# The last two chunks of a feed-forward projected up by seven products of halves

## The chip, the cores and the metric

The kernel runs on one core of a Trainium2 chip. The metric is the device time of one execution in microseconds; before the change the median of three runs is 2227.38 us. The engines named here are TensorE (PE in the profile, its weight loads PEld), VectorE (DVE), ScalarE (ACT), GpSimd (POOL) and SyncE (SP, which issues most loads).

## The reference, cut to what matters

The network has two layers over 512 tokens of width 1024. Each layer has a SwiGLU feed-forward, a mixer, a second feed-forward and a gated embedding, and after each of them a normalised residual. The change is in the feed-forwards, of which there are four; hidden width is 2816.

```
def swiglu_ffn(x, w_gu, w_d):
    g, u = jnp.split(x @ w_gu, 2, axis=-1)
    return (jax.nn.silu(g) * u) @ w_d
...
x = layer_norm(DN_ALPHA * x + 0.5 * swiglu_ffn(x, ffn1_wgu[i], ffn1_wd[i]), ln_g[i, 0], ln_b[i, 0])
```

Everything is float32.

## The kernel before, in words

**Float32 by three products.** A float32 operand is kept as two parts, a high part that is rounded to the matmul's type by a ScalarE copy, and a low part, the rest, which VectorE makes by a subtraction (`split`, and lines 198 and 207 for weights). `mm3` (lines 279 to 281) makes three matmuls of each product: high by high, high by low, low by high. So each weight tile costs one ScalarE and one VectorE instruction of 128 x 1024 elements before TensorE may use it.

**One feed-forward.** The hidden width is 22 blocks of 128, taken in chunks of 2, 4, 4, 4, 4 and 4 blocks (`FFN_CHUNKS`; chunk 0 to chunk 5). For each block there are two projections up, gate and up half: 8 input blocks by three matmuls of 512 tokens, 24 matmuls into one PSUM bank (`up`, the tile fps). ScalarE applies Silu to the gate (sg), VectorE multiplies it by the up half into h. The activations stand transposed in xh and xl (high and low part, 8 input blocks by 512 tokens).

**The product down** of a chunk is done one chunk later, woven into the next chunk's projections, by the class `Group`: seven products of halves (a Strassen form) in place of eight. Each product needs one form of h (`form`: VectorE sums, then a split into fhi and flo) and one form of the down weights (kind "rows", `forms`). One product is 12 matmuls of 512 columns (the tile gps), and its result is added to the residual xt by two VectorE additions (`add`). The order in a chunk is: projection, product, projection, product, and so on, seven products within eight projections. The last chunk's down product is not woven: it is plain rows of weights after the chunk (`down`, the tile dps).

**Weights.** The class `Weights` holds an order of all weight tiles, and splits the next one when a buffer is free. There are four buffers of kind "main" and three of kind "rows". `release` after a product gives a buffer back and at once issues the split of the tile that is next in the order, so a tile's split is issued when the product that stands four main tiles ahead has been issued, and waits for that product's matmuls. Raw weights come by DMA into three buffers of 1 MB (wraw) and five of 512 KB (wquarter). Elsewhere in the kernel, in the mixers, `release(low="dma")` makes the low part without VectorE: ScalarE writes the negated copy, and a GpSimd DMA adds the raw weights to it in place (line 205).

**What sets the order.** Every engine's queue is written out by the program (`manual_schedule`): instructions stand in the order in which the Python code calls them, and wait on semaphores for what they read and overwrite. There are four banks for projections and four for the down side.

Of the kernel before, what the change touches and what calls it, by code (L numbers as in the profile page):

```python
# [10 lines left out]
F32 = mybir.dt.float32  # L11
# [33 lines left out]
PLE_EXTRA = 3  # L45


class Weights:
# [4 lines left out]
    def __init__(self, nc, raw_pool, split_pool):  # L53
        self.nc = nc
        self.pools, self.free = {"main": split_pool}, {"main": W_BUFS, "none": 0}
        self.raw_pools, self.raw_bufs = {"raw": raw_pool}, {"raw": RAW_BUFS}
        self.raw_free, self.raw_at, self.raw_tags = deque(range(RAW_BUFS)), {}, {}
        self.loads, self.left, self.raws = [], [], {}
        self.queues, self.held_raws = defaultdict(deque), defaultdict(deque)
        self.order, self.next_split, self.in_place = [], 0, set()  # L60
        self.ready, self.taken, self.held = deque(), deque(), []
# [34 lines left out]
    def forms(self, kind, b11, b12, b22, b21):  # L96
# [25 lines left out]
        return [(kind, js, make) for js, make in made]  # L122

# [50 lines left out]
    def fill(self, most=1000, low=None, meanwhile=None):  # L174

        while most and self.next_split < len(self.order):
# [19 lines left out]
            for i in range(parts):  # L196
                s = slice(i * shape[1] // parts, (i + 1) * shape[1] // parts)
                self.nc.scalar.activation(hi[:, s], src[:, s], AF.Copy)  # L198
                if meanwhile and make in self.in_place:
                    meanwhile()  # L200
                    meanwhile = None
                if low == "dma" and make not in self.in_place:

                    self.nc.scalar.activation(lo[:, s], src[:, s], AF.Copy, scale=-1.0)
                    self.nc.gpsimd.dma_start(lo[:, s], src[:, s], accum_op=OP.add)
                else:
                    self.nc.vector.tensor_sub(lo[:, s], src[:, s], hi[:, s].bitcast(F32))  # L207
# [41 lines left out]
def hybrid_trunk(ctx: ExitStack, tc, x, p, ln_g, ln_b, ffn1_wgu, ffn1_wd, ffn2_wgu, ffn2_wd,  # L249
# [39 lines left out]
    def up_bank(name):  # L289
        up_order.rotate(-1)  # L290
        return ps_up.tile([P, 512], F32, name=name, tag=f"up{up_order[-1]}")
# [56 lines left out]
    LAST = len(FFN_CHUNKS) - 1  # L348
    turn_p = []

    def ffn_weights(wgu, wd, name, ple=False):
# [12 lines left out]
        for at in range(HB):  # L364
            if at in (0, HB - 1):
                W.add(*((kp(wgu)[:, :, c0:c0 + P], [slice(None)]) for c0 in (at * P, HID + at * P)))
            elif at % 2:
                add_pairs(wgu, at * P, HID + at * P)
        tiles = W.order[first:]
        del W.order[first:]  # L370
        for c, n in enumerate(FFN_CHUNKS):
            down_w = deque(forms(c - 1) if c else ())
            for i in range(2 * n):
# [5 lines left out]
        add_rows(wd, starts[LAST], 4, ["rows", "rows", "main", "main"] if ple else ["main", "rows", "rows", "rows"])  # L379
# [74 lines left out]
    def ple_weights(i):  # L454
        add_rows(ple_wp[i], 0, 2)
        add_wide(ple_wg[i], 0, ["extra", "extra", "extra", "main"])
        add_wide(ple_wg[i], 512, ["rows", "rows", "rows", "rows2"])
# [196 lines left out]
    def down(hs, first, norm=None, lazy=False, defer=False):  # L654
# [5 lines left out]
        def release(k):  # L660
            kind = "rows" if kinds[k] == "rows" else None
            if norm is None:
                W.release(kind=kind)
            elif kind == "rows":
# [162 lines left out]
    def ffn(layer, k, rows, prepare=None):  # L827
        with stage_pool("forms", 2) as fpool, stage_pool("quarters", Q_BUFS) as qpool, stage_pool("hpool", 2) as hpool:
# [14 lines left out]
            group, hs = None, []  # L843
            for c, n in enumerate(FFN_CHUNKS):
# [4 lines left out]
                for i in range(2 * n):  # L849
# [20 lines left out]
                    if c == 1 and i < 3:  # L870
                        run_affine()
                if c < LAST:
# [5 lines left out]
                if c == 1:  # L878
                    norm = Norm(layer, k)
            return down(hs, False, norm, lazy=layer == 0, defer=prepare is not None)  # L880

    def ffn_stage(layer, k):
        with stage_pool("rows", 3) as rows:
            W.open("rows", rows, 3)
            ffn(layer, k, rows)
            W.close("rows")

# [572 lines left out]
    def ffn_ple(i, last):  # L1460
        with stage_pool("rows", 3) as rows:
            W.open("rows", rows, 3)
# [18 lines left out]
            finish = ffn(i, 2, rows, load_p)  # L1481
            with stage_pool("extra", PLE_EXTRA) as extra, stage_pool("rows2") as rows2, stage_pool("ple2") as mp:
# [68 lines left out]
                for kind in ("rows", "rows2", "extra"):  # L1551
# [55 lines left out]
```

## Time and profile before

| | before |
|---|---|
| median of 3 runs | 2227.38 us (2226.92 to 2227.43) |
| profiled execution, span | 2225.4 us, granted TensorE clock 0.999 |
| TensorE busy | 2214.4 us in 10517 matmuls |
| VectorE, ScalarE, GpSimd busy | 1557.3, 922.2, 104.3 us |
| VectorE and ScalarE, 214.5 to 340 us (chunks 4 and 5 of the first feed-forward) | 80.5 and 44.2 of 125.5 us |
| moved by DMA | 253.57 MB, mean 114 GB/s |

A row of a group or of the timeline names line, engine, operation, output and inputs (buffer numbers left out), and shapes; a timeline row begins with its start and its duration in microseconds, and a bracket at its end gives the idle time ahead of it and who ended it. Matmuls overlap, so their price is the distance between two starts, not their duration. In the answers by windows each row has the stretch, its length, the busy time of TensorE, its weight loads, VectorE, ScalarE and GpSimd (with counts), the granted clock, the mean busy share of the 16 DMA engines, and GB/s.

### The profile page before, as it was taken

What the parts mean: (1) busy time and instruction counts of PE and PEld (TensorE: products, weight loads), DVE (VectorE), ACT (ScalarE), POOL (GpSimd) and SP (SyncE); (2) the same over time, 40 slices, a digit from 0 to 9 for tenths busy, and PEclk for the clock granted to TensorE, in tenths of its full rate; (3) what the DMA queues carried; (4) which work ended last, traced back from release to release, by engine and by line L of the source; (5) the groups of instructions that cost most, each with busy time, mean ns of one, the idle gap of its engine ahead of it and who ended that gap; (6) DMA issues with size and microseconds to landing.
All of it is one profiled execution on the core that took longest, in us unless ns stands there. A gap on an engine that the chain in (4) does not pass through costs nothing.

```text
span 2225.4 us, 26475 instructions
## 1 busy us (share of the span) xinstructions
PE 2214.4 (100%) x10517; PEld 1856.1 (83%) x10517; DVE 1557.3 (70%) x2280; ACT 922.2 (41%) x1308; POOL 104.3 (5%) x135
## 2 busy tenths in 40 slices
PE   9999999999999999999999999999999999999998
PEld 8888888888888888888888888888888888888887
DVE  5666667776776786666687766666788778666677
ACT  4333336464646443333345333335345453333332
POOL 1000000111101100000000000000001100000000
PEclk9999999999999999999999999999999999999999
DMA  7422223466847444332233422223437743332221
GB/s 230 130 95 88 95 86 100 100 143 140 160 117 154 130 133 128 98 106 63 99 123 111 134 92 90 95 85 97 140 76 152 164 129 130 117 114 86 85 86 57
DMA packets 206308, 253.57 MB, mean 114 GB/s; under 512 B 5812, under 2 KB 160564, under 8 KB 206184
## 3 DMA queue, kind: packets, MB, share of 16 engines
q1 hardware_dynamic: 168080, 211.83, 29.4%
q0 software_dynamic: 31488, 25.35, 8.4%
q10 hardware_dynamic: 6616, 14.69, 2.0%
q8 instruction: 83, 1.36, 0.2%
q14 instruction: 41, 0.34, 0.0%
HBM read 224.58 MB, written 2.11 MB: 102 GB/s over the span
## 4 chain that ended last, share of the span: by engine, by line
PE 98%; ACT 1%; DMA 0%; DVE 0%; issue 0%; SPq 0%; DVEq 0%
PE fps L279 13%; PE fps L280 13%; PE fps L281 13%; PE gps L279 8%; PE gps L281 8%; PE gps L280 8%; PE dps L279 2%; PE dps L281 2%; PE dps L280 2%; PE gups L279 1%; PE vps L279 1%; PE zps L279 1%; PE zps L281 1%; PE vps L281 1%; PE gvps L279 1%; PE gups L280 1%
## 5 line engine op out<-in xcount | busy, mean ns | idle before, releaser
L279 PE MATMUL fps<-xh,whi 128*128 128x512 f32 x1312 | 510.7, 389 | 0.0
L280 PE MATMUL fps<-xl,whi 128*128 128x512 f32 x1312 | 510.4, 389 | 0.0
L281 PE MATMUL fps<-xh,wlo 128*128 128x512 f32 x1312 | 510.4, 389 | 0.0
L207 DVE TENSOR_TENSOR wlo<-wraw,whi 128x1024 fp32r<-128x1024 f32 (+1 forms) x292 | 352.7, 1218 | 147.9 <-ACT whi L198 146.8
L198 ACT ACTIVATE whi<-wraw 128x1024 fp32r<-128x1024 f32 (+1 forms) x340 | 352.2, 1048 | 179.0 <-PE fps L280 81.6
L207 DVE TENSOR_TENSOR wlo<-wquarter,whi 128x1024 fp32r<-128x1024 f32 (+1 forms) x140 | 156.5, 1118 | 218.2 <-ACT whi L198 218.2
L281 PEld LDWEIGHTS fps<-xh,wlo 128*128 128x128 f32 x1312 | 246.2, 188 | 51.3
L279 PEld LDWEIGHTS fps<-xh,whi 128*128 128x128 f32 x1312 | 246.3, 188 | 51.2
L280 PEld LDWEIGHTS fps<-xl,whi 128*128 128x128 f32 x1312 | 246.3, 188 | 50.6
L198 ACT ACTIVATE whi<-wquarter 128x1024 fp32r<-128x1024 f32 (+1 forms) x140 | 136.3, 974 | 279.8 <-PE gps L281 209.0
L281 PE MATMUL gps<-whi,flo 128*128 128x512 f32 x644 | 251.1, 390 | 0.0
L279 PE MATMUL gps<-whi,fhi 128*128 128x512 f32 x644 | 251.1, 390 | 0.0
L280 PE MATMUL gps<-wlo,fhi 128*128 128x512 f32 x644 | 251.0, 390 | 0.0
L628 DVE TENSOR_TENSOR xt<-xt,gps 128x512 f32<-128x512 f32 x302 | 193.2, 681 | 0.7 <-PE gps L281 0.7
L856 ACT ACTIVATE sg<-fps 128x512 f32<-128x512 f32 x80 | 47.9, 598 | 228.5 <-PE fps L281 224.3
L281 PEld LDWEIGHTS gps<-whi,flo 128*128 128x128 f32 x644 | 120.9, 188 | 25.7
L280 PEld LDWEIGHTS gps<-wlo,fhi 128*128 128x128 f32 x644 | 120.9, 188 | 25.5
L279 PEld LDWEIGHTS gps<-whi,fhi 128*128 128x128 f32 x644 | 120.9, 188 | 25.5
L284 ACT ACTIVATE fhi<-h 128x512 fp32r<-128x512 f32 (+1 forms) x140 | 80.5, 581 | 142.8 <-DVE h L793 54.4
L285 DVE TENSOR_TENSOR flo<-h,fhi 128x512 fp32r<-128x512 f32 (+1 forms) x140 | 87.2, 635 | 42.9 <-ACT fhi L284 42.9
L598 POOL TENSOR_TENSOR rs<-rs,eps_pow 128x1 f32<-128x1 f32 x32 | 20.6, 643 | 1573.6 <-DVE rs L597 1573.6
L501 ACT ACTIVATE xf<-xps,cols 128x128 f32<-128x128 f32 x160 | 59.8, 454 | 53.5 <-PE xps L496 53.5
(306 smaller groups left out, 3625.8 us busy)
## 6 DMA issues: line engine op xcount, KB each, us to landing
wraw<-in_ffn_wgu_dram SPq DMA_DIRECT2D x79, 1024.0 KB, 6.3
wquarter<-in_ffn_wd_dram SPq DMA_DIRECT2D x64, 512.0 KB, 3.7
wraw<-in_ml_w_in_dram SPq DMA_DIRECT2D x24, 1024.0 KB, 5.5
wlo<-wraw POOLq DMA_DIRECT2D x48, 512.0 KB, 6.6
wraw<-in_gm_w_in_dram SPq DMA_DIRECT2D x15, 1024.0 KB, 5.6
wraw<-in_ffn_wgu_dram SPq DMA_DIRECT2D x17, 512.0 KB, 4.0
wraw<-in_ffn_wd_dram SPq DMA_DIRECT2D x8, 1024.0 KB, 4.9
wraw<-in_ml_w_out_dram SPq DMA_DIRECT2D x8, 1024.0 KB, 5.0
```

The costliest lines, as they stand in the source:

```text
L198: self.nc.scalar.activation(hi[:, s], src[:, s], AF.Copy)
L207: self.nc.vector.tensor_sub(lo[:, s], src[:, s], hi[:, s].bitcast(F32))
L279: mm(ps, st[0], mv[0], start=start, stop=False, skip_group_check=more)
L280: mm(ps, st[0], mv[1], start=False, stop=False, skip_group_check=more)
L281: mm(ps, st[1], mv[0], start=False, stop=stop, skip_group_check=more)
L284: sca.activation(hi, src, AF.Copy)
L285: vec.tensor_sub(lo, src, hi.bitcast(F32))
L501: sca.activation(xf[:, k], ps[:, k], AF.Identity, scale=col("ln_g", norm.at + 4 * g + k), bias=col("ln_b", norm.at + 4 * g + k))
L598: pool.tensor_tensor(rs[:, 1:2], rs[:, 0:1], eps_pow, op=OP.pow)
L628: vec.tensor_add(dst, dst, ps)
L856: sca.activation(sg, ps, AF.Silu)
```

## The change

In chunks 4 and 5 (`UP_FROM = 4`) the projections up are done by seven products of halves too. The matrices that are halved: the weights of two blocks, with gate and up half as the two column halves, and the two halves of the 1024 inputs as the row halves; the activations, halved over inputs and over the 512 tokens. One pair of blocks takes seven products in place of four projections. A product is 2 blocks by 4 input blocks by three matmuls, of 256 tokens: 24 matmuls (the tile ups, `UpPair.product`). The order in a chunk becomes 14 products with a down product after the first and every second one: product 0, down, 1, 2, down, 3, 4, down, and so on.

- *Weights* (`up_forms`): of the seven forms two are sums and differences of two VectorE instructions (s2) and one each (s3, s4), made in place in the raw tile; three are quarters as loaded, and s1 is what s2 left. Forms 1, 2, 4, 5 and 6 (`UP_BY_DMA`) get their low part by ScalarE's negated copy and an accumulating GpSimd DMA, forms 0 and 3 by VectorE.
- *Activations* (`UpForms`): four transformed quarters, t1 to t4, each with high and low part, made once for each feed-forward while chunk 3 runs, two steps at each projection from the fourth on; the rest, `last`, stands after chunk 3's last projection. The third, t3, takes the place of a quarter of xh and xl; t1 takes the buffer of gamma and beta, so these are loaded (`Norm`) at the end of chunk 5 and no longer in chunk 1.
- *Results* (`UpPair.take`): products share two or three banks; ScalarE copies a bank out after products 0, 2 and 3, VectorE adds after 1, 4 and 5, ScalarE applies Silu after 1 and 5, VectorE multiplies after 5 and 6.
- *Buffers*: two "rows" and one "rowsx", which is opened at the end of chunk 5 from the memory of t2, in place of three "rows"; a bank can be held.

How this stands in the engines' queues, in the first feed-forward. First VectorE at the end of chunk 3, from the h of the last projection (L860 before, L1057 now) on. Before:

```order
L860 SCALAR_TENSOR_TENSOR h<-sg,fps 128x512
L207 TENSOR_TENSOR wlo<-wraw,whi 128x1024
L285 TENSOR_TENSOR flo<-h,fhi 128x512 x2
L114 TENSOR_TENSOR wquarter<-wquarter 128x1024
L115 TENSOR_TENSOR wquarter<-wquarter 128x1024
```

Now, with x_d, x_f and x_wlo for sums of activations and the t tiles for transformed quarters (t3's low part is the row that writes xl):

```order
L1057 SCALAR_TENSOR_TENSOR h<-sg,fps 128x512
L246 TENSOR_TENSOR wlo<-wraw,whi 128x1024
L324 TENSOR_TENSOR xl<-x_wlo,xh 128x4x256
L900 TENSOR_TENSOR x_d<-xh,xl 128x512
L931 TENSOR_TENSOR x_d<-x_d,x_f_1300 128x512
L900 TENSOR_TENSOR x_d<-xh,xl 128x512
L931 TENSOR_TENSOR x_d<-x_d,x_f_1300 128x512
L932 TENSOR_TENSOR t_wlo<-x_f_1300,t_whi 128x1024
L324 TENSOR_TENSOR t_f_1754<-x_d,t_f_1753 128x512 x2
L324 TENSOR_TENSOR flo<-h,fhi 128x512 x2
```

Between h and the low parts of the first forms of h (flo), which the first down products of chunk 4 read, one row stood before; now eight do. On TensorE the first down product (12 matmuls gps) stood after the 24 matmuls of 512 tokens of chunk 4's first projection; now it stands after the 24 matmuls of 256 tokens of the first product.

Then VectorE from product 12 of chunk 4 on (us is the copy of a bank, wraw the raw weights in which L139 and L140 make s2):

```order
L975 TENSOR_TENSOR us<-us,ups 128x512
L989 SCALAR_TENSOR_TENSOR h<-us 128x2x256
L139 TENSOR_TENSOR wraw<-wraw 128x1024
L140 TENSOR_TENSOR wraw<-wraw 128x1024
L246 TENSOR_TENSOR wlo<-wquarter,whi 128x1024
L687 TENSOR_TENSOR xt<-xt,gps 128x512 x2
L989 SCALAR_TENSOR_TENSOR h<-us,ups 128x2x256
L246 TENSOR_TENSOR wlo<-wraw,whi 128x1024
L324 TENSOR_TENSOR flo<-h,fhi 128x512 x2
```

The first form of chunk 4's h now stands behind the form s2 of the next chunk's weights and a row's low part; before, the same rows as in the first fence stood there. ScalarE's queue at this place, where before a projection had one copy of 128 x 1024 (whi), has for most products two, whi and the negated wlo:

```order
L237 ACTIVATE whi<-wraw 128x1024
L243 ACTIVATE wlo<-wraw 128x1024
L237 ACTIVATE whi<-wquarter 128x1024
L237 ACTIVATE whi<-wraw 128x1024
L323 ACTIVATE fhi<-h 128x512 x2
L972 ACTIVATE us<-ups 128x512
```

The high part of a row (wquarter) stands behind both copies of a weight that is used later.

The diff, cut to its core:

```diff
+UP_BY_DMA = (1, 2, 4, 5, 6)
...
+    def up_forms(self, g, u):
+        vec = self.nc.vector
+        def quarter(j, k):
+            return self.raws[j][:, 4 * k:4 * k + 4]
...
+        def s2():
+            vec.tensor_add(quarter(u, 0), quarter(u, 0), quarter(u, 1))
+            vec.tensor_sub(quarter(g, 0), quarter(u, 0), quarter(g, 0))
+            return quarter(g, 0), (g,)
...
+        def s3():
+            vec.tensor_sub(quarter(u, 0), quarter(u, 1), quarter(g, 0))
+            return quarter(u, 0), (u,)
+        def s4():
+            vec.tensor_sub(quarter(g, 1), quarter(g, 1), quarter(g, 0))
+            return quarter(g, 1), (g,)
...
+        made = [((g,), a11), ((), a12), ((u,), s2), ((), s1), ((), s3), ((), s4), ((), a22)]
...
+        self.by_dma.update(made[r][1] for r in UP_BY_DMA)
...
-                if low == "dma" and make not in self.in_place:
+                if make in self.by_dma or low == "dma" and make not in self.in_place:
                     self.nc.scalar.activation(lo[:, s], src[:, s], AF.Copy, scale=-1.0)
                     self.nc.gpsimd.dma_start(lo[:, s], src[:, s], accum_op=OP.add)
...
+            def last():
+                split(*self.t3, b)
+                d = [tmp_tile("x_d").rearrange("p (k t) -> p k t", k=2) for _ in range(2)]
+                for i, s in enumerate(halves):
+                    joined(d[i], 1, 0, s)
+                    vec.tensor_sub(d[i], d[i], c[:, s])
+                vec.tensor_sub(f32r(self.t2, late, "wlo"), c, self.t2[0].bitcast(F32))
+                hi, lo = f32r(self.t4, pool, "f1"), f32r(self.t4, pool, "f0")
+                for i, s in enumerate(halves):
+                    split(hi[:, s], lo[:, s], d[i])
...
+        def product(self, r):
+            w = W.take()
+            c = (0, 1, 0, 3, 0, 3, 0)[r]
...
+            for e in range(2):
+                for k in range(4):
+                    mm3(ps[:, e], [a[:, k, e * P:(e + 1) * P] for a in w], [a[:, k] for a in self.right[r]],
+                        r == c and e == 0 and k == 0, k == 3, r != c or e > 0)
+        def take(self, r):
+            bank, part = self.bank, self.part
+            if r in (0, 2, 3):
+                part[r] = tmp_tile("us").rearrange("p (e c) -> p e c", e=2)
+                sca.activation(part[r], bank[3 if r == 3 else 0], AF.Copy)
+            elif r in (1, 5):
+                g = part[r // 5 * 2]
+                vec.tensor_add(g, g, bank[1 if r == 1 else 3])
+                sca.activation(g, g, AF.Silu)
+                if r == 5:
+                    self.gated(1, g, part[3])
+            elif r == 4:
+                vec.tensor_add(part[3], part[3], bank[0])
+            else:
+                self.gated(0, part[0], bank[0])
...
+            def up_products(c, n, h):
...
+                for s in range(7 * n // 2):
+                    b, r = s // 7 * 2, s % 7
+                    if r == 0:
+                        pair = UpPair(formed, None if h is None else h[:, b:b + 2])
+                    pair.product(r)
+                    group.add()
...
+                    pair.take(r)
+                    W.release()
+                    if s % 2 == 0:
+                        group.product()
+                        W.release(kind="rows")
+                        group.form()
...
+                if c == UP_FROM - 1:
+                    while formed.steps:
+                        formed.step()
+                    formed.last()
                 if c < LAST:
                     group = Group(h, fpool, c == 0)
                     group.form()
                     group.form()
```

145 lines of the change are left out of this document (122 added, 23 removed).

## The prediction, made before the result was known

> **What bounds the kernel now.** I read the page's first part, then its chain, then who TensorE waits for.
>
> ```profile
> span 2225.4 us, 26475 instructions
> PE 2214.4 (100%) x10517; PEld 1856.1 (83%) x10517; DVE 1557.3 (70%) x2280; ACT 922.2 (41%) x1308; POOL 104.3 (5%) x135
> PE 98%; ACT 1%; DMA 0%; DVE 0%; issue 0%; SPq 0%; DVEq 0%
> PE sup L731 <- DVE wlo L207: 0.4, 1, 0.4
> ```
>
> TensorE is 98% of the chain, and its largest wait for another engine's data after the start is 0.4 us. Two consequences: matmul time removed is removed from the span, one for one; and every microsecond for which TensorE is made to wait is added, one for one. There is no other slack to draw on. So the sum has two terms: matmul time, and new waits.
>
> **Term 1, matmul time.** Matmuls overlap in the pipeline, so their mean of 389 ns is not their price; the distance between starts is. First row to last in each piece, from the timeline:
>
> ```profile
> 253.86 0.39 PE L279 MATMUL fps<-xh,whi 128*128 128x512 f32 x1
> 259.30 0.39 PE L279 MATMUL gps<-whi,fhi 128*128 128x512 f32 x1
> ...
> 251.14 0.39 PE L279 MATMUL gps<-whi,fhi 128*128 128x512 f32 x1
> 253.86 0.39 PE L279 MATMUL fps<-xh,whi 128*128 128x512 f32 x1
> ...
> 375.40 0.28 PE L279 MATMUL sup<-xh,whi 128*128 128x256 f32 x1
> 378.28 0.28 PE L279 MATMUL sup<-xh,whi 128*128 128x256 f32 x1
> ```
>
> One projection (24 matmuls of 512 columns) takes 5.44 us, one product of the down group (12) 2.72, and 24 matmuls of 256 columns 2.88: 0.120 us each, not half of 0.227. Chunks 4 and 5 of one feed-forward now hold 16 projections, 16 x 5.44 = 87.04 us. The change puts 4 pairs x 7 products x 24 matmuls of 256 columns there: 28 x 2.88 = 80.64. That is 6.4 us less per feed-forward, 25.6 us in all (an eighth would have been 10.9; the shorter matmul gives back 4.5). The 14 down products stay.
>
> **Term 2, what is added to VectorE and ScalarE.** Their distances between starts, and the hand-overs:
>
> ```profile
> 213.06 0.39 PE L279 MATMUL fps<-xh,whi 128*128 128x512 f32 x1
> 213.84 0.68 DVE L860 SCALAR_TENSOR_TENSOR h<-sg,fps 128x512 f32<-128x512 f32 x1
> 214.44 1.22 DVE L207 TENSOR_TENSOR wlo<-wraw,whi 128x1024 fp32r<-128x1024 f32 x1
> 215.58 1.28 DVE L285 TENSOR_TENSOR flo<-h,fhi 128x512 fp32r<-128x512 f32 x2
> 216.78 1.22 DVE L114 TENSOR_TENSOR wquarter<-wquarter 128x1024 f32<-128x1024 f32 x1
> 218.03 1.22 DVE L115 TENSOR_TENSOR wquarter<-wquarter 128x1024 f32<-128x1024 f32 x1
> ...
> 213.08 1.06 ACT L198 ACTIVATE whi<-wraw 128x1024 fp32r<-128x1024 f32 x1 [1.61 <-PE fps L280]
> 214.05 1.20 ACT L284 ACTIVATE fhi<-h 128x512 fp32r<-128x512 f32 x2
> ...
> 250.71 0.69 DVE L285 TENSOR_TENSOR flo<-h,fhi 128x512 fp32r<-128x512 f32 x1 [0.76 <-ACT fhi L284]
> 251.32 1.28 DVE L628 TENSOR_TENSOR xt<-xt,gps 128x512 f32<-128x512 f32 x2
> ...
> 214.50:277.00 62.50, 62.50 (x278) 51.74 (x277) 40.42 (x49) 21.62 (x27) 0.00 (x0) 1.00 0.26 85
> 277.00:340.00 63.00, 63.00 (x280) 52.16 (x279) 40.11 (x50) 22.57 (x30) 0.00 (x0) 1.00 0.29 94
> ```
>
> VectorE: 0.60 us for 512 columns, 1.14 for 1024, 1.25 where one needs the one ahead. ScalarE: 0.97 and 0.60. A result passes to another engine in about 0.07 (0.76 for a 0.62 us copy between two VectorE steps). In chunks 4 and 5 (windows) VectorE is busy 80.5 of 125.5 us. Built, the change has 47 VectorE instructions of 1024 columns and 74 of 512 there: 47 x 1.14 + 74 x 0.60 = 98 us beside 80.64 + 14 x 2.72 = 118.7 us of TensorE, 83%, plus the gaps in which it waits for ScalarE. That fits as an average. But an engine keeps its order: at 250.71 VectorE idles 0.76 us for ScalarE's copy, though the residual add behind it (251.32) needs only a product that ended long before. So what counts is what stands ahead of the item that TensorE needs, at three places.
>
> *Place A, chunk 3 to 4.* Before, after the last projection (213.06) TensorE had a whole projection, 5.44 us, before a down product needed the first h form; VectorE's queue to it was h, one weight low part, two low parts: done by 216.86, with 2.1 us to spare (5.44 + 2 x 0.227 - 3.80). Now only one product (2.88) stands between, and the form's low part is needed at the third matmul: 3.33 us after the projection's end. In VectorE's queue stand h, one weight low part, xl (third transformed half; it overwrites an activation quarter that the last projection still reads, so no idle time before can take it), four x_d, t_wlo, two t_f, and only then flo: 0.60 + 1.14 + 1.14 + 0.60 + 0.70 + 0.60 + 0.70 + 1.14 + 1.20 + 0.69 = 8.5, from 0.2 on, 8.7 us. Stall at least 8.7 - 3.3 = 5.4. Filling the queue backwards with the same prices, VectorE reaches h only at 1.6: a row weight's high part on ScalarE waits for the slot that the down product frees at -5.44 and stands behind the two copies of another weight until -3.4; low part, two x_a, two t1, two residual adds follow (1.14 + 1.2 + 1.35 + 1.2). So 6.8. I take 6.8, bounds 5.4 and 6.8.
>
> *Place B, chunk 4 to 5.* From the end of product 12, T: VectorE has to add us (0.8), wait for ScalarE's Silu (1.5), gate (2.2), two weight forms (4.7), wait for ScalarE's two copies of that form and a row's high part (7.7), its low part (8.9), two residual adds (10.1), gate (10.8), a low part (11.9), then flo: 12.7. TensorE needs it at T + 2.72 + 2.88 + 2.88 + 0.45 = 8.9. Stall 3.8 with a VectorE that comes to T on time; by the queue from A on it comes 2.2 us late, since four row forms and ScalarE's order (two large copies per product) hold it up. I take 6.0, bounds 3.8 and 6.0.
>
> *Place C, chunk 5 to the down rows.* From product 12: add, Silu, gate and split 3.6, four low parts of the last rows to 8.6, adds 9.8, gate 10.4, ScalarE's high part 11.1, low part 11.9. The rows' third block needs it at 2.72 + 2.88 + 2 x 1.36 + 0.45 = 8.8. Stall 3.1; both bounds near.
>
> *Inside the chunks* the queues give four waits of 1.2 to 1.3 us (TensorE adds into a bank that ScalarE copies out late) and two of 1.7 and 2.4 (the s2 form's low part), 9.1 in sum. They come out of a hundred added-up steps, so I take half, 4.6, bounds 0 and 9.1.
>
> **The accumulating DMAs** cost TensorE nothing if they land in time; before, the same kind lands so:
>
> ```profile
> 565.00:590.00 25.00, 25.00 (x111) 20.49 (x110) 20.64 (x31) 16.55 (x22) 2.54 (x3) 1.00 0.54 134
> DMA to landing us min/median/max: 4.5/4.8/6.0
> ...
> 595.00:606.00 11.00, 11.00 (x50) 9.02 (x49) 4.64 (x9) 5.66 (x9) 4.39 (x6) 1.00 1.32 207
> DMA to landing us min/median/max: 9.7/11.2/12.7
> ```
>
> 4.8 us where GpSimd issues in 0.85 us (whole rows), 11.2 in a burst of column pieces. The change's quarters are whole rows of 4 KB, and five per 30 us; I use 4.8 to 5. The slot of a product r+4 is freed by product r; it is needed 3 products and 2 down products later, 3 x 2.88 + 2 x 2.72 = 14.1 us. The longest chain (add, Silu, gate, two forms, two copies, landing) is 0.8 + 0.7 + 0.7 + 2.5 + 2.1 + 5 = 11.8. Covered by 2.3 us; without the cover, TensorE waits. The 15.4 us of forming activations in chunk 3 otherwise lie in VectorE's 22 idle us; two row buffers for three, and gamma and beta loaded later, I cost at nothing: a row's slot frees 13.6 us ahead of its use, and the loads have the down rows ahead of them.
>
> **The sum per feed-forward**: 6.8 + 6.0 + 3.1 + 4.6 = 20.5 us of waits against 6.4 gained: 14.1 longer, four times 56.4. 2225.4 + 56.4 = 2281.8; the median of runs lies 2.0 above this profiled span (2227.4), so **2284 us**. With all low bounds 12.3 - 6.4 = 5.9, +24, 2251; with all high ones 25 - 6.4 = 18.6, +74, 2302.
>
> **The rivals.**
> *Only the queues' least* (2251 us): VectorE catches up inside the chunks, since 17% of it is free. For it the average; against it ScalarE's order.
> *Faster* (2202 us): the burst at A is hidden, and the gain of 25.6 stands. One mechanism: VectorE and ScalarE absorb the new forms in time that is idle now (22 of 62.5 us). For it the windows above, and that A, B and C need only be under 6.4 us together; against it xl, which cannot start before the last projection ends, and 8.5 us of queue behind it. It decides when flo is ready under 9.7 us after the last projection and B and C vanish.
> *They cancel* (2223 to 2232): the waits come to 5.3 to 7.5 us per feed-forward.
> *The low parts come late* (2350): landings of 11.2 instead of 4.8 overrun the cover of 2.3 by 4.1 us, 16 pairs: +66 on the forecast. For it the burst above, at a DMA share of 1.32; against it the whole rows.
> *The clock falls* (2298): TensorE's own start shows what an idle array costs:
>
> ```profile
> 1.43 3.68 PE L1560 MATMUL warm<-ident 128*128 128x128 f32 x16 [1.43 <-POOL ident masks.py:199]
> 6.87 1.26 PE L1560 MATMUL warm<-ident 128*128 128x128 f32 x10
> ```
>
> After idling 16 matmuls take 3.68 us, later ten take 1.26, so 16 would take 2.0: 1.7 us lost. If A and B each do this, 8 x 1.7 = 14 us more. The profile before grants 1.00 throughout and has no such wait, so it cannot say. [...]
>
> **How the numbers follow.** Forecast 0.47, least queues 0.18, clock 0.14, late low parts 0.05, cancel 0.05, faster 0.11. Below 0.2% (4.5 us) a measurement of this kernel cannot tell from no change. Faster 0.11, same 0.05, slower 0.84. The likeliest case's own range is 2251 to 2302; the range for 8 in 10 takes in half of the cancelling case and the clock: 2226 to 2315.
>
> **What would show it.** TensorE waiting for flo (line 324) and fhi at the first down product of chunk 4, 5 to 7 us, four times; the same at chunk 5; matmuls ups at 0.120 us; VectorE near 80 to 85% in chunks 4 and 5. I am wrong if the waits of TensorE sum to under 40 us, if ups come at over 0.125, or if PEclk dips account for more than the waits do.

## The result, and the profile after

The changed kernel takes 2334.61 us (median of 4 runs, 2333.58 to 2336.45), the kernel before 2227.27 us beside it: ratio 1.0484, 95% interval 1.0469 to 1.0499. It is 4.8% slower; 2284 us was forecast, with a range up to 2315. The profiled execution has a span of 2332.2 us, 106.8 more than before.

Busy times from the page of the changed kernel:

```profile
PE 2231.4 (96%) x11669; PEld 1909.1 (82%) x11669; DVE 1678.9 (72%) x2436; ACT 1081.3 (46%) x1508; POOL 172.5 (7%) x215
```

Before, TensorE was busy 2214.4 of 2225.4 us. So the 106.8 us split in two: idle time of TensorE grew from 11.0 to 100.8 us (+89.8), and its busy time grew by 17.0 us, where 25.6 us less had been worked out. Whom TensorE waited for (sum, times, longest):

```profile
PE gps L318 <- ACT fhi L323: 34.9, 8, 5.5
PE dps L318 <- ACT wquarter L323: 21.5, 4, 5.8
PE gps L320 <- DVE flo L324: 11.6, 8, 2.4
PE ups L318 <- ACT us L972: 9.1, 14, 1.3
PE ups L320 <- DMA wlo<-wraw: 8.6, 8, 2.1
PE ups L318 <- DVE us L989: 4.3, 4, 1.3
```

These six make 90.0 us. The first and the third are the form of h at places A and B, the second is place C, the other three (22.0 us) lie inside the chunks. Place A in the first feed-forward, from the timeline: the last projection's end, h and its two forms, and the down product.

```profile
212.67 0.39 PE L320 MATMUL fps<-xh,wlo 128*128 128x512 f32 x1
...
214.61 0.68 DVE L1057 SCALAR_TENSOR_TENSOR h<-sg,fps 128x512 f32<-128x512 f32 x1
...
220.78 1.13 ACT L323 ACTIVATE fhi<-h 128x512 fp32r<-128x512 f32 x2
221.45 0.80 PE L318 MATMUL gps<-whi,fhi 128*128 128x512 f32 x1 [5.53 <-ACT fhi L323]
...
222.66 1.29 DVE L324 TENSOR_TENSOR flo<-h,fhi 128x512 fp32r<-128x512 f32 x2
223.41 0.80 PE L320 MATMUL gps<-whi,flo 128*128 128x512 f32 x1 [0.73 <-DVE flo L324]
...
224.00 0.63 PE L318 MATMUL gps<-whi,fhi 128*128 128x512 f32 x1
224.43 0.63 PE L319 MATMUL gps<-wlo,fhi 128*128 128x512 f32 x1
```

The queue did what it had been read to do: h 1.7 us after the projection's end, and its forms 6 and 8 us behind it; 5.53 + 0.73 = 6.3 us of waiting where 6.8 was forecast. But the last two rows show something else: matmuls of 512 columns now start 0.43 us apart, not 0.227. Three stretches around the waits at A, B and C, and one between the first two (columns: stretch, length, busy time of TensorE, weight loads, VectorE, ScalarE, GpSimd, granted clock, DMA share, GB/s):

```profile
212.90:223.40 10.50, 4.25 (x27) 3.32 (x25) 10.33 (x15) 4.79 (x7) 0.00 (x0) 0.74 0.00 0
223.40:285.00 61.60, 60.38 (x403) 55.42 (x404) 43.20 (x52) 33.92 (x41) 7.56 (x9) 0.96 0.66 158
285.00:300.00 15.00, 9.61 (x39) 7.76 (x38) 10.13 (x12) 8.59 (x10) 1.69 (x2) 0.66 0.42 104
...
358.40:375.00 16.60, 10.76 (x40) 8.39 (x39) 11.46 (x15) 4.59 (x6) 0.24 (x1) 0.79 0.68 236
```

The granted clock falls at all three places and recovers between them. Its record has 12 stretches at half rate between the start and the end, three in each feed-forward, 88.7 us together; for 26.3 us of these TensorE idles in any case. VectorE is busy for 43 of 62 us in chunk 4, 70%, where the prediction named 80 to 85% as a sign: it has room on average, and is late all the same.

### The profile page after: what moved, and what is told of

It reads as the page before. It is cut to its first block, busy times and chain, and to the rows that moved or that the text cites. A ratio compares the mean times of both kernels' runs of the same rounds, so it can differ in the third digit from the quotient of the medians.

```text
span 2332.2 us, 29478 instructions
## 1 busy us (share of the span) xinstructions
PE 2231.4 (96%) x11669; PEld 1909.1 (82%) x11669; DVE 1678.9 (72%) x2436; ACT 1081.3 (46%) x1508; POOL 172.5 (7%) x215
## 5 line engine op out<-in xcount | busy, mean ns | idle before, releaser
L237 ACT ACTIVATE whi<-wraw 128x1024 fp32r<-128x1024 f32 (+1 forms) x388 | 400.1, 1047 | 193.4 <-DVE wraw L140 50.4
L318 PE MATMUL fps<-xh,whi 128*128 128x512 f32 x800 | 311.4, 389 | 0.0
L319 PE MATMUL fps<-xl,whi 128*128 128x512 f32 x800 | 311.2, 389 | 0.0
L320 PE MATMUL fps<-xh,wlo 128*128 128x512 f32 x800 | 311.2, 389 | 0.0
L320 PE MATMUL gps<-whi,flo 128*128 128x512 f32 x644 | 258.8, 402 | 11.6 <-DVE flo L324 11.6
L319 PE MATMUL gps<-wlo,fhi 128*128 128x512 f32 x644 | 258.3, 401 | 0.0
L244 POOL DMA_DIRECT2D wlo<-wraw x128 | 127.8, 998 | 1560.5 <-ACT wlo L243 1406.2
L318 PEld LDWEIGHTS fps<-xh,whi 128*128 128x128 f32 x800 | 150.2, 188 | 31.2
L319 PEld LDWEIGHTS fps<-xl,whi 128*128 128x128 f32 x800 | 150.2, 188 | 31.1
L320 PEld LDWEIGHTS fps<-xh,wlo 128*128 128x128 f32 x800 | 150.1, 188 | 31.1
L318 PE MATMUL ups<-xh,whi 128*128 128x256 f32 x512 | 146.6, 286 | 6.4 <-DVE us L989 4.3
L320 PE MATMUL ups<-xh,wlo 128*128 128x256 f32 x512 | 146.5, 286 | 2.3 <-DMA wlo<-wraw 2.1
L319 PEld LDWEIGHTS gps<-wlo,fhi 128*128 128x128 f32 x644 | 125.3, 195 | 24.9
L319 PE MATMUL ups<-xl,whi 128*128 128x256 f32 x512 | 145.5, 284 | 0.0
```

The source lines that it names most:

```text
L318: mm(ps, st[0], mv[0], start=start, stop=False, skip_group_check=more)
L319: mm(ps, st[0], mv[1], start=False, stop=False, skip_group_check=more)
L320: mm(ps, st[1], mv[0], start=False, stop=stop, skip_group_check=more)
```

## The experiments

Each was timed in three rounds beside the kernel before, which took 2227.0 to 2227.1 us in these rounds. Diffs are against the changed kernel unless they say otherwise.

**1. The forms of h ahead of the last sums.** The prediction's place A as a matter of order alone.

```
                 if c == UP_FROM - 1:
                     while formed.steps:
                         formed.step()
-                    formed.last()
                 if c < LAST:
                     group = Group(h, fpool, c == 0)
                     group.form()
                     group.form()
+                if c == UP_FROM - 1:
+                    formed.last()
```

> Only the order at the end of chunk 3 is changed: the two first forms of h are issued before the rest of the activation forms (last), not behind them. Theory 1: the wait at place A (5.5 us for fhi and 1 to 2 for flo, four times, some 27 us) falls to under 6 us in sum and its four clock drops (about 8 to 10 us of half clock each, 17 us in sum) go: 2290 to 2300 us. Some of it may come back at product 2, which needs the t2 low part. Theory 2: the same work stands in the same queues, so the wait moves to products 2 and 4: above 2320 us.

Measured 2340.24 us, ratio 1.0508 (1.0492 to 1.0523). TensorE's waits:

```profile
PE ups L318 <- ACT us L972: 35.9, 18, 6.9
...
PE gps L318 <- ACT fhi L323: 13.8, 4, 3.7
```

The four waits for fhi at A are gone, and four waits of 6.9 us for the copy of a product's bank (us) stand in their place. That is the second theory: order alone moves the wait, and whatever stands behind the last sums is late.

**2. The same with the seventh sum put off, the next group's forms early, and the token halves swapped.**

```
+                    if c == UP_FROM and s == 1:
+                        formed.fourth()
+                    if c < LAST and s == 10:
+                        nxt = Group(h, fpool)
+                    if c < LAST and s in (10, 12):
+                        nxt.form()
```

> Three changes of order, no change of work: the first forms of h before the rest of the activation forms, of which t4 comes only after product 1; the first two forms of chunk 4's h issued after its products 10 and 12 in place of after 13; the two token halves swapped, so that product 5 and not 6 finishes the tokens that the forms and the down rows read first. Theory 1: A, B and C fall to under 2 us each, the clock stays at 1.00, what is left are the waits inside the chunks (22 us in the changed kernel): 2227 - 25.6 + 22 = about 2224 us, 2215 to 2240. Theory 2: the waits move into the chunks: above 2280 us.

Measured 2309.28 us, ratio 1.037 (1.0353 to 1.0388): 25 us better than the change, 82 worse than before, so again the second theory. The wait at A is up to 4.6 us now, again for the bank's copy, and at B TensorE waits for VectorE to read a bank:

```profile
PE ups L318 <- ACT us L974: 35.8, 22, 4.6
PE ups L318 <- DVE h L991: 11.6, 4, 4.0
```

**3. Only chunk 5 by seven products.**

```
-    UP_FROM = 4
+    UP_FROM = 5
```

> UP_FROM is 5: only the last chunk is projected by seven products, the activations are formed in chunk 4. Gain of matmul time halves to 12.8 us. Theory 1: places A and C remain whole (27 and 22 us), B goes, the waits inside the chunk halve (11 us), two of three clock drops remain (30 us): 2227 - 12.8 + 27 + 22 + 11 + 30 = about 2304 us. Theory 2: the loss goes with the number of products: half of 107 us, about 2280 us.

Measured 2304.82 us, ratio 1.035 (1.0334 to 1.0365), as the first theory had it. The burst of sums moves to the turn before chunk 5 and costs there what it cost at A, 5.5 us each; the waits at the down rows stay:

```profile
PE gps L318 <- ACT fhi L323: 22.1, 4, 5.5
PE dps L318 <- ACT wquarter L323: 20.0, 4, 6.3
```

**4. Useless products in the waits**, to keep the clock up. First with the next bank in turn:

```
                     pair.product(r)
+                    if s == 0:
+                        busy(BUSY)
                     group.add()
...
+                if late_half and t == 0 and k == 2:
+                    busy(BUSY)
```

> Three times in each feed-forward, right where TensorE waits longest (before the first down product of chunk 4, of chunk 5, and before the third block of the down rows), 22 useless matmuls of 512 columns (22 x 0.227 = 5.0 us) are added that read only finished activations; nothing else changes, the result neither. Theory 1 (order): the three waits are set by VectorE's and ScalarE's queues, so the added work fills them and costs nothing, and what it saves is the price of the clock alone. In the changed kernel the granted clock stood at one half for 88.7 us outside the end; at full use that is 44 us. Expected: granted clock 1.00, 2334.6 - 44 = about 2290 us (2283 to 2300). Theory 2 (load): VectorE and ScalarE have too much to do in chunks 4 and 5, and the slow clock only overlaps with waits that would come anyway: clock 1.00, but 2320 to 2335 us.

Measured 2345.72 us, ratio 1.0534 (1.0515 to 1.0553). The useless products took a bank out of its turn, and TensorE waited for banks instead (`PE ups L319 <- DVE us L997` 15.5 us, `PE junk L347 <- DVE h L997` 12.3), so this run says nothing on the clock. Repeated with a bank that stands free:

```
-        bank = up_bank("junk")
+        i = [i for i in up_order if i not in up_held][at]
+        bank = ps_up.tile([P, 512], F32, name="junk", tag=f"up{i}")
```

> The changed kernel, with 22 useless 512-column products (22 x 0.227 = 5.0 us at full clock) ahead of the first down product of chunks 4 and 5 and of the down rows, as in the run before with such products, but now written into a bank of PSUM that stands free, so that the turn of the banks stays as it was. If the clock's fall is a price of its own (88.7 us of the profiled execution at half rate, some 44 us lost): the clock is 0.995 or more, the waits left behind the useless products are the 90 us of the changed kernel less what the products fill, and the time is about 2334.6 - 44 = 2290 us. If TensorE at half clock only waits less later, because VectorE and ScalarE catch up in that time: the clock is as high, but the other waits grow, and the time is 2320 to 2335 us.

Measured 2337.58 us, ratio 1.0496 (1.048 to 1.0512). The clock was kept: 0.996 in place of 0.980. Neither expectation is met, though the second is close. Its busy times, and TensorE's largest wait:

```profile
PE 2270.8 (97%) x11933; PEld 1943.2 (83%) x11933; DVE 1679.3 (72%) x2436; ACT 1081.5 (46%) x1508; POOL 172.8 (7%) x215
```

```profile
PE ups L319 <- ACT us L981: 15.0, 19, 1.3
```

The useless products cost 264 x 0.227 = 60 us and took busy time from 2231.4 to 2270.8, 39 us: some 20 us of clock were won. TensorE's idle time fell from 100.8 to 63.6, 37 us. So 60 - 37 = 23 us of useless products lay outside the old waits or made way for new ones (the waits for us, for the bank and for the DMA inside the chunks grew from 22.0 to 37 us), which ate the 20 won. A faster TensorE meets its late partners sooner; not all that the clock lost can be won back.

**5. and 6. The clock by itself**, in the kernel before, whose VectorE has room at that place: useless adds ahead of chunk 4's first form (8, and 15).

```
                         run_affine()
+                if c == 3:
+                    extra = tmp_tile("extra")
+                    for _ in range(8):
+                        vec.tensor_add(extra, xt[:, 0, :512], xt[:, 1, :512])
                 if c < LAST:
                     group = Group(h, fpool, c == 0)
```

> The kernel before, with 8 useless adds of 512 columns (about 0.60 us each) on VectorE ahead of the first low form of h at the turn from chunk 3 to chunk 4, in each of the four feed-forwards. The form has 2.1 us of cover there, so TensorE should wait 8 x 0.60 - 2.1 = 2.7 us for it, 11 us in all. If a wait as short as this leaves the clock alone: clock 1.00, 2227 + 11 = 2238 us. If each wait of this size halves the clock for the 6.8 us seen in the changed kernel: 4 x 3.4 = 14 us more, 2252 us, clock 0.994. If the adds have more cover than thought: 2227 us and no wait.

> The same with 15 adds: TensorE should wait 15 x 0.60 - 2.1 = 6.9 us per feed-forward, 28 us in all, about as long as the changed kernel waits at that place. Nothing else of the kernel is changed. If the clock falls behind every such wait as in the changed kernel (6.8 to 10.2 us at half rate, 3.4 to 5.1 us lost): 2227 + 28 + 14 to 20 = 2269 to 2275 us, clock 0.991 to 0.994. If the fall of the clock belongs to the changed kernel's products and not to the wait: 2255 us, clock 1.00.

Measured 2244.97 us (ratio 1.0077, 1.006 to 1.0093) with 8, and 2268.11 us (1.0184, 1.0169 to 1.0199) with 15. The wait with 8, then the wait with 15 and matmuls behind it, 0.42 us apart:

```profile
PE gps L281 <- DVE flo L285: 11.6, 4, 2.9
```

```profile
PE gps L281 <- DVE flo L285: 31.9, 4, 8.0
```

```profile
226.91 0.80 PE L281 MATMUL gps<-whi,flo 128*128 128x512 f32 x1 [7.98 <-DVE flo L285]
...
227.93 0.63 PE L280 MATMUL gps<-wlo,fhi 128*128 128x512 f32 x1
228.35 0.63 PE L281 MATMUL gps<-whi,flo 128*128 128x512 f32 x1
```

The spans grew by 18.9 and 40.2 us, the waits make 11.6 and 31.9. So 7.3 and 8.3 us are the clock's, with the fraction of a microsecond that each fresh start costs: 1.8 us for each wait of 2.9 us, 2.1 for each of 8.0. The granted clock is 0.996 with 8 adds and 0.991 with 15, where it was 0.999; behind the first wait of 2.9 us, too, matmuls start 0.43 us apart. A wait is paid once while it lasts and then by about 2 us more, and 2.9 us were enough. The fall belongs to the wait, not to the change's products.

**7. Without the last sums.** The burst at A is left out.

```
-                lambda: sca.activation(f32r(self.t2, late, "whi"), c, AF.Copy), t1, split_t1]
+                lambda: sca.activation(f32r(self.t2, late, "whi"), c, AF.Copy), lambda: self.t2.append(self.t2[0]), t1, split_t1]
...
-                          self.quarter(1, 1), self.t4]
+                          self.quarter(1, 1), self.t1]
...
-                    formed.last()
```

> The changed kernel without the burst that forms the last of the sums ahead of chunk 4: the fifth, third and seventh product get stand-ins that are there already, so t3 and t4 are not formed and the low part of t2 is not; the output is not the reference's for that reason, the products and their number are the same. If the burst (some 6.1 us of VectorE work ahead of the first low form, 2.2 us on ScalarE) makes the long wait at chunk 4: its wait of 8.6 us per feed-forward goes to under 2, and so does the fall of the clock behind it (4 x 3.4 = 14 us): 2334.6 - 27 - 14 = 2294 us. If VectorE's whole load about chunk 4 sets the time, and the burst only shows where it is paid: the wait comes back at the products' bank copies, and the time falls by VectorE's work alone, 4 x 6.1 = 24 us at most: 2310 us or more.

Measured 2311.88 us, ratio 1.0378 (1.0362 to 1.0393): 22.7 us less. A's wait is gone as the first theory had it, but the time follows the second:

```profile
PE dps L318 <- ACT wquarter L323: 21.7, 4, 8.4
PE gps L318 <- ACT fhi L323: 14.4, 4, 4.9
...
PE dps L318 <- ACT whi L237: 7.9, 2, 3.9
```

B is much as it was (23.3 us for fhi and flo, after 21.5), and the wait at the down rows has grown from 21.5 to 29.6 us: part of what A gave back is paid there.

**8. Without any sums.** Products, banks and combining stay; quarters as loaded stand in for the sums of the weights, and for those of the tokens with their high and low parts.

```
         def s3():
-            vec.tensor_sub(quarter(u, 0), quarter(u, 1), quarter(g, 0))
             return quarter(u, 0), (u,)
...
+            self.steps, self.last = [], lambda: None
```

> The changed kernel with Strassen's seven products per pair, their banks and the combining of the results, but without any of the sums ahead of them: neither the sums of the weights nor those of the tokens are formed, loaded quarters stand in for them, and the output is not the reference's for that reason. The products' own gain was forecast at 25.6 us. If VectorE's added work makes the waits: they fall from 90 to some 30 us (the products' bank copies 13, the accumulating DMAs 9, the forms of h at the turns of the chunks 8), and the time is about 2227 - 26 + 30 + 8 for the clock = 2239 us. If the waits at chunk 5 and at the down rows come from late loads and from the order of the queues, they stay (21 and 21 us) beside the 22 us of copies and DMAs: 2227 - 26 + 64 + 18 = 2283 us.

Measured 2232.74 us, ratio 1.0026 (1.0016 to 1.0036). The sums, 130 us of VectorE and 17 of ScalarE, cost 102 us; nothing else in the change is dear but the wait at the down rows, the only one left of over 0.3 us behind the start. Busy times and that wait:

```profile
PE 2201.6 (99%) x11669; PEld 1896.2 (85%) x11669; DVE 1548.9 (69%) x2296; ACT 1064.4 (48%) x1484; POOL 172.6 (8%) x215
```

```profile
PE dps L314 <- ACT wquarter L319: 18.4, 4, 5.9
```

The accumulating DMAs, all there, make no wait here. And the products' gain can be read: TensorE is busy 12.8 us less than before, though the granted clock is 0.994 in place of 0.999. That difference of 0.005 in a span of 2231 us is 11 us; so up to some 24 us less at full clock (an estimate), against 25.6 forecast.

**9. and 10. The sums of the tokens alone, and those of the weights alone.** The first fence is the edit for the tokens' sums alone: it takes out the weights' four sums per pair, two for s2 and, not shown, one each for s3 and s4. The second is that for the weights' alone.

```
-            vec.tensor_add(quarter(u, 0), quarter(u, 0), quarter(u, 1))
-            vec.tensor_sub(quarter(g, 0), quarter(u, 0), quarter(g, 0))
```

```
+            self.right = [q(0, 0), q(1, 0), q(0, 1), q(1, 1), q(0, 1), q(1, 1), q(0, 0)]
+            self.steps, self.last = [], lambda: None
```

> The changed kernel without the sums of the weights (64 VectorE operations of 1.22 us, 78 us; loaded quarters stand in, so the output is not the reference's), the sums of the tokens as they are (130 - 78 = 52 us of VectorE). If the costs add up and the weights' sums carry most: 2232.7 us (neither sum) + the 6.3 us of waits at chunk 4 and some 2 of clock in each feed-forward = 2266 us, with the waits at chunk 5 gone. If the two hurt only together: under 2250 us. If the tokens' sums carry nearly all of the 102 us: over 2310 us.

> The changed kernel without the sums of the tokens (stand-ins for the five sums, so the output is not the reference's), the sums of the weights as they are. If the costs add up: 2334.6 - 33 = 2301 us, the long waits at chunk 4 gone and those at chunk 5 as they were. If the two hurt only together: under 2270 us. If the weights' sums cost little: 2240 us.

Measured 2265.56 us (ratio 1.0174, 1.0157 to 1.0191) with the tokens' sums and 2303.52 us (1.0344, 1.0329 to 1.036) with the weights'. Over 2232.7 that is 32.8 and 70.8 us, 103.6 together, where both at once cost 101.9: they add up, and both times are within 3 us of the first expectation. The waits with the tokens' sums alone:

```profile
PE dps L314 <- ACT wquarter L319: 18.7, 4, 6.0
PE gps L314 <- ACT fhi L319: 18.6, 4, 4.7
PE gps L316 <- DVE flo L320: 3.0, 4, 0.8
```

and the weights' alone:

```profile
PE dps L318 <- ACT wquarter L323: 19.9, 4, 5.8
PE gps L318 <- ACT fhi L323: 14.8, 4, 5.1
PE ups L318 <- ACT us L973: 12.6, 18, 1.5
PE ups L320 <- DMA wlo<-wraw: 10.0, 8, 2.4
PE gps L320 <- DVE flo L324: 9.1, 4, 2.6
```

The tokens' sums make place A (21.6 us of waits, the rest the clock), the weights' sums make place B and the waits inside the chunks, those for the DMA too. Place C needs neither.

**11. The last splits behind the last h.** Place C: in the changed kernel the last h stands on VectorE behind two low parts, whose high parts wait on ScalarE for a load of the mixer's weights:

```profile
361.30 2.00 ACT L237 ACTIVATE whi<-wraw 128x1024 fp32r<-128x1024 f32 x2 [1.88 <-DMA wraw<-in_ml_w_in_dram]
362.38 2.36 DVE L246 TENSOR_TENSOR wlo<-wraw,whi 128x1024 fp32r<-128x1024 f32 x2 [1.53 <-ACT whi L237]
...
365.86 0.68 DVE L989 SCALAR_TENSOR_TENSOR us<-us,ups 128x512 f32<-128x512 f32 x1
367.26 0.80 PE L318 MATMUL dps<-whi,wquarter 128*128 128x512 f32 x1 [5.84 <-ACT wquarter L323]
```

```
-                    W.release()
+                    end = c == LAST and b == n - 2
+                    if not (end and r == 5):
+                        W.release()
+                    if end and r == 6:
+                        W.release()
+                        W.release(kind="rows")
```

> The changed kernel; in the last pair the splits of the next weights that follow the sixth product are issued behind the last h instead of ahead of it. In the trace of the changed kernel the last h of the first feed-forward starts 7 us after its bank is there, because two low parts (2.36 us) that wait for a load, and an add (1.28 us), stand ahead of it on VectorE. If this queue makes the wait of 5.4 us ahead of the down rows: it falls to about 3 us (add, h, split: 0.6 + 0.7 + 0.7 and their starts), 4 x 2.4 = 10 us, and some of the clock's fall: 2335 - 10 to 15 = 2320 to 2325 us. If the down rows' own weights are what is late: they wait for those instead, and the time stays at 2335 us or rises.

Measured 2321.36 us, ratio 1.0424 (1.0408 to 1.044): 13.2 us less, as the queue had it. The waits at the down rows fell from 21.5 to 7.7 us:

```profile
PE dps L318 <- ACT whi L237: 4.8, 2, 2.4
...
PE dps L319 <- DVE wlo L246: 2.9, 4, 0.8
```

**12. All low parts on VectorE**, no accumulating DMA for these weights.

```
-UP_BY_DMA = (1, 2, 4, 5, 6)
+UP_BY_DMA = ()
```

> The changed kernel with all seven low parts of a pair on VectorE, none by accumulating DMA: 80 more VectorE subtractions of 1.22 us (98 us in all), 80 fewer ScalarE copies of 1.04 us, no accumulating DMA for them. If VectorE's work sets the time in chunks 4 and 5: 2335 + some 60 to 98 = 2395 to 2433 us. If late loads and the order of the queues set it, VectorE has room (it is busy 43 of 62 us in chunk 4) and ScalarE's queue gets shorter: 2320 to 2345 us, the waits for the DMA (8.6 us) gone.

Measured 2361.91 us, ratio 1.0605 (1.0589 to 1.062): between the two expectations, 27 us more for 92 us more of VectorE and 73 less of ScalarE:

```profile
PE 2236.2 (95%) x11669; PEld 1916.7 (81%) x11669; DVE 1771.2 (75%) x2516; ACT 1008.1 (43%) x1428; POOL 104.8 (4%) x135
```

So the DMAs do earn their place, and a microsecond of VectorE has no one price: 0.30 us for these low parts (27.3 of 92.3, with ScalarE relieved), 0.59 for the sums of the tokens (32.8 of 56.0, with 16 us of ScalarE added), 0.97 for those of the weights (70.8 of 73.1).

**13. The sums of the weights on GpSimd**, which stands idle for 93%.

```
     def up_forms(self, g, u):
-        vec = self.nc.vector
+        vec = self.nc.gpsimd
```

> The changed kernel with the sums of the weights on GpSimd, which is busy 7% of the time, instead of VectorE; nothing is left out. What GpSimd takes for one is not in any trace so far; VectorE takes 1.22 us. If VectorE's queue is what makes them dear and GpSimd takes up to twice as long: 2334.6 - 30 to 60 = 2275 to 2305 us. If the chain from a load over the sum to the split is what makes them dear, or if GpSimd takes three times as long or more: 2335 us or more, with waits of the products for whi and wlo.

Measured 2391.74 us, ratio 1.0741 (1.0725 to 1.0757), the slowest of all, though the sums left VectorE's queue: above the first expectation, as the second had it. Two of the four sums on GpSimd (groups: busy time and mean ns of one, then idle time ahead); two of VectorE's groups, which had 1118 and 631 ns in the changed kernel; and from the timeline one of VectorE's adds beside one of GpSimd's:

```profile
L147 POOL TENSOR_TENSOR wraw<-wraw 128x1024 f32<-128x1024 f32 x16 | 50.0, 3126 | 49.8 <-DVE wlo L246 42.7 <-ACT us L972 7.0
...
L140 POOL TENSOR_TENSOR wraw<-wraw 128x1024 f32<-128x1024 f32 x16 | 40.8, 2553 | 1.3
...
L111 DVE TENSOR_TENSOR wquarter<-wquarter 128x1024 f32<-128x1024 f32 (+1 forms) x20 | 33.9, 1694 | 0.7
...
L856 DVE TENSOR_TENSOR h<-h 128x512 f32<-128x512 f32 (+1 forms) x20 | 29.9, 1497 | 0.0
...
229.44 4.05 DVE L111 TENSOR_TENSOR wquarter<-wquarter 128x1024 f32<-128x1024 f32 x1
229.75 2.64 POOL L151 TENSOR_TENSOR wraw<-wraw 128x1024 f32<-128x1024 f32 x1
```

GpSimd takes 2.5 to 3.1 us for what VectorE does in 1.22. VectorE as a whole is busy 1669.5 us, where it is 1604.9 without the weights' sums (run 9): 65 us more. The row of L111 above took 4.05 us beside a sum on GpSimd, where the group's mean in the changed kernel was 1.12. Two things changed at once, the longer way from a load over the sum to the split, and a slower VectorE, and this run can't tell their shares apart.

**14. One chunk with all mends**: the edits of 2 and 11, and this one.

```
-    UP_FROM = 4
+    UP_FROM = 5
```

> Only the last chunk by the seven products (that alone was 2304.8 us), with the mends together: the forms of h ahead of the last sums, the seventh sum after the first product, the halves of the tokens swapped, the last splits behind the last h. Theory of the queues: the wait at chunk 5 (5.5 us per feed-forward) and part of that at the down rows go, 4 x (4 + 2.4) = 26 us and some 5 of the clock: 2275 us. Theory of VectorE's work: the waits move to the products' copies as they did with both chunks, 2290 to 2300 us. Faster than before (2227 us) by neither: the products' gain is 12.8 us, and the bank copies, the DMAs and the last latency cost more.

Measured 2281.33 us, ratio 1.0244 (1.0229 to 1.0259), between the two expectations and the best of the versions that compute everything; slower than before by 54 us. Of its waits the largest is the bank's copy, behind the sums of the tokens again:

```profile
PE ups L318 <- ACT us L974: 23.7, 10, 4.6
```

No version beats the kernel before.

## Why the prediction was wrong

The direction and the mechanism of the waits held; the size did not: +56.4 us was forecast, +106.8 came in the profiled spans. Step by step:

- *Waits, right.* Forecast 20.5 us per feed-forward, 82 in all; idle time of TensorE grew by 89.8. A 6.8 against 6.3 measured. B 6.0: the two rows for fhi and flo make 46.5 us, less A's 6.26 x 4 leaves 21.5, 5.4 each. Inside the chunks 4.6 against 22.0 / 4 = 5.5, in part by luck: the 4.6 was half of a sum that the author did not trust. Only C was short: 3.1 against 21.5 / 4 = 5.4, because two low parts ahead of the last h wait for a load; run 11 put them behind it.
- *The clock, the step that failed.* The sum had no term for it. It stood as a rival of chance 0.14, priced at 14 us. But it is no alternative to the forecast: the waits forecast at A and B, 6.3 and 5.4 us as measured, came with a fall in each of the four feed-forwards. Busy time grew by 17.0 us where 25.6 less was forecast, 42.6 us apart. The trace says where they lie, matmul by matmul (from one start to the next, without the idle time, less the usual distance of its shape). The 142 that start at half rate, 0.427 us apart in place of 0.227, or 0.213 in place of 0.120, cost 28.6 us, the first ones behind waits among them. The stops and starts at the waits cost 12.6 more: the last matmul ahead of an idle gap counts with its whole length, 0.39 us for 512 columns where 0.227 is usual (9.9 us in 50 gaps), and the first behind one is followed 0.1 us late (2.7 us outside the half rate). The remaining 1.4 us are open. So three things were wrong in the price of 14 us: C was not counted among the places (12 falls, not 8); a fall costs 28.6 / 12 = 2.4 us (a wait of runs 5 and 6 paid 1.8 and 2.1, the fresh start with it), not the 1.7 read off the start; and the stops and starts had no price.
- *Product gain, right*: 25.6 forecast, some 24 estimated from run 8; the distance of 0.120 us holds.

The balance: 7.8 us of waits too few, and 42.6 us of busy time (17.0 + 25.6), nearly all of it the half rate and the stops and starts: 50.4 us, which is 106.8 - 56.4.

The trace of the changed kernel shows where the falls lie. Of its 12 stretches at half rate one lasts 3.4 us, eight 6.8 and three 10.2, and all begin on one grid of 3.413 us. The step of this grid ahead of each fall holds 1.95 to 3.41 us of idle time of TensorE; of the steps at full clock with no fall behind them none holds more than 1.86. Thirteen waits of over 2 us began at full clock. Twelve, of 3.05 to 5.84 us, brought a fall; at A in the first feed-forward it came 1.95 us into the wait. One, of 2.13 us for a DMA (to 2232.02 us), brought none: it lay across a border of the grid, 1.86 and 0.27 us to its sides.

Of the rivals, the late low parts came to little (8.6 us, and none in run 8). The view that VectorE absorbs the forms in its idle time falls with runs 8 to 10: at 72% busy it lost 102 us for 130 us of added sums. The test named for being wrong, waits under 40 us, a distance over 0.125 us, or more lost to the clock than to waits, shows none of the three (90 us, 0.120 us, 28.6 us); it left out that both terms come at once.

What stays open is why sums of weights cost nearly their whole length and low parts a third. ScalarE's rows point to the place, but do not show it: ahead of its high parts it idled 50.4 us for one of the weights' sums (the row below, of the changed kernel), and in its queue behind them stand the copies on which TensorE waits. No run moved the sums alone to a place where nothing waits.

```profile
L237 ACT ACTIVATE whi<-wraw 128x1024 fp32r<-128x1024 f32 (+1 forms) x388 | 400.1, 1047 | 193.4 <-DVE wraw L140 50.4
```

## What to carry to other kernels

Where TensorE is 98% of the chain, a Strassen form must pay for its sums: here 7/8 of the products in smaller matmuls gained some 24 us, and 130 us of sums on an engine that was 70% busy cost 102. A wait of TensorE of 2.9 us cost its length and 1.8 us more for the clock and the fresh start behind it, one of 8.0 us 2.1 more (runs 5 and 6): price this as a term of the same sum. A wait at the end of a full queue mostly moves when the order is mended (runs 1 and 2) and even when work leaves the queue (run 7, in part); it goes when what stands ahead of it waits for something that is not needed yet, and is put behind (run 11).

## What the runs showed of the hardware

With nothing but useless adds put into the kernel before, four waits of TensorE of 2.9 us made the span 18.9 us longer, 7.3 more than the waits themselves, and four of 8.0 us 40.2 longer, 8.3 more; the granted clock was 0.996 and 0.991, where it was 0.999. In the trace of the changed kernel the clock fell to half rate twelve times, each time behind a step of a grid of 3.413 us in which TensorE idled 1.95 us or more; behind steps at full clock with up to 1.86 us it did not fall. GpSimd added 128 x 1024 float32 elements in 2.5 to 3.1 us, VectorE in 1.22 (group means), and in the run in which GpSimd did so two groups of VectorE had means of 1694 and 1497 ns in place of 1118 and 631. Not all groups rose: the residual adds of a PSUM bank (xt<-xt,gps) took 679 ns in the mean in both kernels, and L116, of the same shape as L111, 1119 in both. What slowed the two groups is not shown.
